# First FFN of a diffusion backbone: five of seven modulation sums move from TensorE to trees of accumulating DMAs

## The chip, the cores and the metric

One core of one Trainium2 chip. The metric is the device time in microseconds of one execution of the whole program. TensorE is called PE, VectorE DVE, ScalarE ACT, GpSimd POOL and SyncE SP, as in the profile.

## The reference

Two layers over 256 latent tokens (`x`) and, in layer 0, 256 context tokens (`ctx`); width 1024, FFN width 2816. Each layer is a half-step SwiGLU FFN, a token mixer (neighbourhood attention, then a short convolution) and a second FFN. Everything is FP32. Cut to what the change touches:

```python
m  = (silu(c)     @ ada_w[i] + ada_b[i]).reshape(B, 9, 1, D)   # nine modulation vectors for x
mc = (silu(c_ctx) @ ada_w[i] + ada_b[i]).reshape(9, D)         # and for ctx
# half-step FFN, with shift, scale, gate = m[:, 0], m[:, 1], m[:, 2]
a, u = split((x * (1 + scale) + shift) @ w_in, 2)
y = (silu(a) * u) @ w_out
x = layer_norm(alpha * x + 0.5 * gate * y) * g + b
```

`ada_w[i]` is 1024 x 9216, so the two layers' modulation weights are large, and each is used for a matrix by vector product only.

## The kernel before

**Matmuls.** An FP32 product is made of three passes on PE: weights and activations are each split into a high part (`...h`, rounded to fp32r) and the rest (`...l`), and high x high, low x high and high x low are summed. A weight unit of 512 KB arrives by SP's DMA (`w1r`, `w2r`, `wqr`), ACT copies it to the high part (L216, `w1h`), DVE subtracts to get the low part (L219, `w1l`), each in two halves. The split tiles rotate through five buffers; in the first FFN `ext = [1, 0]` adds a sixth (`whx`, `wlx`).

**First FFN (25 to 398 us).** The 22 blocks of 128 FFN columns come in panels of mostly two blocks; a panel of two blocks has four weight units, each with two of the eight k slices for both gate halves. Three parts follow each other: panels 0 to 3, 4 to 7, 8 to 10. In a part each block j is computed by `f0_mm` (L729): first all k for gate half z = 0, then all k for z = 1; then `f0_gate` (ACT's silu, DVE's product `sil` and the split `gh`, `gl`). After the part's panels, `out_gemm` multiplies by `w_out` (`w2` units, n outside, then the four token tiles t, then units), and DVE adds each result bank to `xt` (`res`, then `x` or `xc`). After the third part comes the layer norm, whose `rs` GpSimd computes (L435, L436), and the attention's query weights `wq`.

**The modulation stream.** `ada(vecs)` computes 14 more modulation vectors in seven groups of two, in the background of the first FFN. For each k slice SP loads `ar` (512 KB, L316), and DVE multiplies by the condition's column and accumulates in `acc` (128 partitions x 1024; L305 first, L307 then), one accumulator for x and one for ctx, or one for each of two vectors. At the end of a group PE sums over the partitions with a matrix `ones` (L342), DVE adds the bias rows (L343, `adar`), and SP stores the rows in `scr` in DRAM (L345), from where later stages load them as `gate` or `mrow`. How fast the stream moves is set by `tick()`, which PE's program calls after pieces of work: it adds the rate `background[1]` to a counter and runs a step of the stream for each whole one. PE's instructions keep the order of the program; for the other engines a scheduler sets it, `queued`, `issue_after` and priorities bind it in places.

**Later groups** (`on_pool`) are summed by GpSimd's PARTITION_ALL_REDUCE and one small DMA to `scr` (L356, L357), five times after 700 us.

Of the kernel before, what the change touches and what calls it, by code (L numbers as in the profile page):

```python
# [10 lines left out]
F32 = mybir.dt.float32  # L11
# [3 lines left out]
ALU = mybir.AluOpType  # L15
# [16 lines left out]
S2 = 7  # L32
WB = (4, 5, 5)
PB = {"mm": 3, "at": 3, "tp": 2}
W_EARLY = 40
ADA_SLOW, ADA_FAST, ADA_SLOWEST = 3, 0.6, 0.13
KT_IDLE = 6
BIAS_AT = 24
ADA_LATE = 20
ADA_LAG = 1  # L40
# [28 lines left out]
E0 = (0,)  # L69
E2 = (0, 5, 7)  # L70
HOLD = 4
SUM_AT = (2, 4, 6, 7, 8)


@with_exitstack
def backbone_kernel(
# [6 lines left out]
    nc = tc.nc  # L83
    sync = nc.sync
# [4 lines left out]
    sp = ctx.enter_context(tc.tile_pool(name="sp", bufs=2))  # L89
# [3 lines left out]
    hp = phase.__enter__()  # L93
# [1 line left out]
    uid = [0]  # L95
    w_early = [0]
    last_split, last_lo = [], []
    ext = [1, 0]
    ada_late = [0]

    def nm(s):
        uid[0] += 1
        return f"{s}_{uid[0]}"
# [7 lines left out]
    def mmb(s="mm", t=0):  # L111
        return bank("at" if t % 2 else "mm", s)
# [11 lines left out]
    background = [None, 0.0, 0.0]  # L124
# [24 lines left out]
    def tick(n=1):  # L149
        clock[0] += n  # L150
        for w in [w for w in waiting if w.due <= clock[0]]:
            w.get()
        background[2] += background[1] * n
        while background[0] is not None and background[2] >= 1:
            background[2] -= 1
            bg_step()
# [122 lines left out]

    for z in mrow:  # L280
        nc.gpsimd.memset(z, 0.0)
    bias_rows = []
    on_pool = [False]
    sums, last_gate = [], []
    gate_ins = []

    def ada(vecs):


        acc = {}  # L290

        def accumulate(l, m, k, w):
            with ExitStack() as st:
                for i in gate_ins + (last_lo if on_pool[0] else []):
                    st.enter_context(tc.issue_after(i.ins))
                for i, vec in enumerate(vecs):
                    if vec[:2] != (l, m):
                        continue
                    if k == 0:
                        acc[i] = hp.tile([P, D], F32, tag="acc", bufs=2, name=nm("acc"))  # L300
                    sc = cst[:, k, vec[2]:vec[2] + 1]
                    for h in range(2):
                        src, a = (c[:, h * 512:(h + 1) * 512] for c in (w, acc[i]))
                        if k == 0:
                            nc.vector.tensor_scalar(a, src, sc, None, op0=ALU.mult)  # L305
                        else:
                            nc.vector.scalar_tensor_tensor(out=a, in0=src, scalar=sc, in1=a,  # L307
                                                           op0=ALU.mult, op1=ALU.add)
            if on_pool[0] and k == KC - 1:
                sums.extend((vec, acc[i]) for i, vec in enumerate(vecs) if vec[:2] == (l, m))  # L310

        loaded = []
        for l, m in dict.fromkeys((l, m) for l, m, _ in vecs):
            for k in range(KC):
                w = hp.tile([P, D], F32, tag="ar", bufs=3, name=nm("ar"))
                sync.dma_start(w, ada_w[l, k * P:(k + 1) * P, m * D:(m + 1) * D])  # L316
                loaded.append((l, m, k, w))
                if len(loaded) > (ADA_LAG if gate_ins else 0):
                    accumulate(*loaded.pop(0))
                yield 1  # L320
        while loaded:
            accumulate(*loaded.pop(0))
            if loaded:
                yield 1
        if on_pool[0]:
            return
        n = 2 * len(vecs)
        if not bias_rows:
            bias_rows.append(hp.tile([P, 512], F32, tag="adab", name=nm("adab")))
            nc.gpsimd.memset(bias_rows[0], 0.0)  # L330
        bt = bias_rows[0]
        for i, (l, m, v) in enumerate(vecs):
            sync.dma_start(bt[64 * i:64 * i + 64:32], ada_b[l, m * D:(m + 1) * D].rearrange("(a b) -> a b", b=512))
        yield 1
        yield 1
        yield 1
        rows = hp.tile([P, 512], F32, tag="adar", name=nm("adar"))
        ps = tpb("ada")
        for i in range(len(vecs)):
            for h in range(2):  # L340
                j = 2 * i + h
                nc.tensor.matmul(ps[32 * j:32 * j + 32, :], ones, acc[i][:, h * 512:(h + 1) * 512], start=True, stop=True)  # L342
        nc.vector.tensor_tensor(out=rows[:32 * n], in0=ps[:32 * n], in1=bt[:32 * n], op=ALU.add)  # L343
        for i, (l, m, v) in enumerate(vecs):
            sync.dma_start(scr[l][v, m * D:(m + 1) * D].rearrange("(a b) -> a b", b=512),  # L345
                           rows[64 * i:64 * i + 64:32, :])
        yield 1

    def sum_up():
# [11 lines left out]
    made = [0]  # L361
# [53 lines left out]
    def residual(ps, xt, gate, wgt, alpha, stats=None, behind=()):  # L415

        t = sp.tile([P, 512], F32, tag="tmp", bufs=3, name=nm("res"))[:, 0:ps.shape[1]]
        with queued(behind[0:1]):
            nc.vector.scalar_tensor_tensor(out=t, in0=ps, scalar=wgt, in1=gate, op0=ALU.mult, op1=ALU.mult)
        with queued(behind[1:2]):  # L420
            if alpha is None:
                nc.vector.tensor_tensor(out=xt, in0=xt, in1=t, op=ALU.add)
            else:
                nc.vector.scalar_tensor_tensor(out=xt, in0=xt, scalar=alpha, in1=t, op0=ALU.mult, op1=ALU.add)
            if stats is not None:
                nc.vector.bn_stats(stats, xt)
# [74 lines left out]
    def run(gen):  # L501
        for _ in gen:
            pass
# [91 lines left out]


    w_in, w_out = ffn_w_in[0, 0], ffn_w_out[0, 0]
    ab0 = hp.tile([P, D], F32, tag="acc", bufs=2, name="ab0")
    nc.vector.memset(ab0, 0.0)
    nc.scalar.dma_start(ab0[2:64:32], ada_b[0, 0:2 * D].rearrange("(m b) -> m b", m=2))  # L600
    xt = []
# [11 lines left out]
    def start_tile():  # L613
        nar[0] += 1
        if nar[0] % 5 in (2, 4):
            return hp.tile([P, 2, 512], F32, tag="pt", bufs=4, name=nm("ar")).rearrange("p a b -> p (a b)")
        return hp.tile([P, D], F32, tag="ar", bufs=3, name=nm("ar"))

    marks = []

# [115 lines left out]
    def f0_gate(bk):  # L736
        t = sp.tile([P, 512], F32, tag="s2", bufs=S2, name=nm("sil0"))
        nc.scalar.activation(t, bk[0], AF.Silu)
        nc.vector.tensor_tensor(out=t, in0=t, in1=bk[1], op=ALU.mult)
        hi, lo = act(F32R, "gh"), act(F32R, "gl")  # L740
        split(t, hi, lo)
        return hi, lo
# [32 lines left out]
    for fh, (p0, p1) in enumerate(parts):  # L775
        gT = []
        for p in range(p0, p1):
            units = u0 if p == 0 else [f0_unit(p, u) for u in range(KC // F0_KN[F0[p][1]])]
            for j in range(F0[p][1]):
                if p == 0:  # L780
                    bk = b0[j]
                else:
                    bk = []
                    for z in range(2):
                        bk.append(mmb("f0", z))
                        for k in range(0, KC, 2):
                            f0_mm(bk[z], p, units, j, z, (k, k + 1))
                            tick()
                gT.append(f0_gate(bk))
        if fh == 0:  # L790
            for v in range(2):
                big = hp.tile([P, 2, 512], F32, tag="pt", bufs=4, name=nm("gate"))
                sync.dma_start(big.rearrange("p a b -> p (a b)"),
                               bass.AP(scr[0].tensor, scr[0][v, 2 * D:3 * D].offset, [[0, P], [1, D]]))
                gates.append([big[:, 0], big[:, 1]])
            background[1] = 0.44
        elif fh == 1:
            ada_late[0] = ADA_LATE

# [281 lines left out]
    hp = phase.__enter__()  # L1081
# [35 lines left out]
    for i in range(len(steps) + LAG + V_LAG):  # L1117
# [14 lines left out]
        n = int(credit)  # L1132
# [28 lines left out]
    phase = tc.tile_pool(name="ph2", bufs=1)  # L1161
    hp = phase.__enter__()
    on_pool[0] = True
    sync.dma_start(scr[1][0, 4 * D:9 * D].rearrange("(a b) -> a b", a=16), ada_b[1, 4 * D:9 * D].rearrange("(a b) -> a b", a=16))
    ext[0] = 2

    v0 = made[0]
# [128 lines left out]
```

## Time and profile before

| | |
|---|---|
| median of 3 runs | 1244.49 us (1244.3 to 1245.33) |
| profiled execution | 1246.53 us |
| its span, first to last instruction | 1244.7 us |
| granted clock | 0.998 |
| PE busy | 1225.9 us, 98% |
| DVE busy | 965.2 us, 78% |
| ACT busy | 643.7 us, 52% |
| POOL busy | 81.6 us, 7% |
| DMA | 275.67 MB, mean 221 GB/s |

The span is cut into stretches in what follows; a stretch's row gives the busy time of each engine in it, and where PE's equals the stretch's length, PE has not waited there. A line such as `L307 DVE ... x266 | 186.6, 747 | 12.3 <-DMA ar` is a group of instructions: busy time, mean ns of one, idle time of the engine just before them and what ended it. Row "a <- b: 10.3, 7, 3.3" of the waits says that an engine waited at a for b: total us, times, longest. Times within PE's timeline are starts; the ends of matmuls overlap.

### The profile page before, as it was taken

To read this page: it belongs to the slowest core of one execution; us is meant where nothing else is said; L and a number is where in the kernel's file an instruction comes from. 1 tells how busy PE (TensorE), PEld (TensorE's weight loads), DVE (VectorE), ACT (ScalarE), POOL (GpSimd) and SP (SyncE) were. 2 spreads that over 40 slices of the span, in tenths; PEclk is the share of its full clock that TensorE was granted. 3 is DMA by queue.
4 is the path that set the end of the run, shared out by engine and by line. 5 is a ranking of instruction groups with operands and counts; after the bars stand their busy time and mean duration, and the time that the engine had idled before them with its cause. 6 is when DMAs were issued, how large, how long until landed. Compare 5 with 4: busy or idle time off the path is not lost.

```text
span 1244.7 us, 17236 instructions
## 1 busy us (share of the span) xinstructions
PE 1225.9 (98%) x5794; PEld 995.3 (80%) x5794; DVE 965.2 (78%) x1675; ACT 643.7 (52%) x1233; POOL 81.6 (7%) x93
## 2 busy tenths in 40 slices
PE   8999999999999999999999999999999999999997
PEld 5787778778778878777788888888888887888886
DVE  3698987888878867888877677878867798768746
ACT  2433132321325566687777635668645644678631
POOL 0000000000001011120000020020200110000200
PEclk9999999999999999999999999999999999999999
DMA  9986679778852654554899957879886765799851
GB/s 294 305 249 228 177 235 298 259 253 289 285 187 68 179 116 95 121 111 128 264 296 311 269 202 242 231 231 324 246 286 225 220 220 153 204 279 277 245 186 68
DMA packets 232304, 275.67 MB, mean 221 GB/s; under 512 B 59622, under 2 KB 178910, under 8 KB 232216
## 3 DMA queue, kind: packets, MB, share of 16 engines
q1 hardware_dynamic: 232020, 274.54, 73.0%
q8 instruction: 45, 0.74, 0.2%
q14 instruction: 43, 0.35, 0.1%
q0 software_dynamic: 160, 0.02, 0.1%
q10 hardware_dynamic: 36, 0.02, 0.0%
HBM read 265.27 MB, written 2.20 MB: 215 GB/s over the span
## 4 chain that ended last, share of the span: by engine, by line
PE 90%; DVE 4%; DMA 3%; ACT 2%; issue 1%; SPq 0%; POOL 0%; DVEq 0%; ACTq 0%
PE f L729 19%; PE w L170 17%; PE w L171 17%; PE w L173 17%; PE wkv L170 3%; PE wkv L171 2%; PE wkv L173 2%; DMA ar<-in_ada_w_dram 1%; PE wc L170 1%; PE wc L171 1%; PE wc L173 1%; PE S L1026 1%; PE o L1064 1%; PE hT L454 1%; PE PT L1051 1%
## 5 line engine op out<-in xcount | busy, mean ns | idle before, releaser
L219 DVE TENSOR_TENSOR w1l<-w1r,w1h 128x512 fp32r<-128x512 f32 (+1 forms) x352 | 232.0, 704 | 44.5 <-ACT w1h L216 43.6
L216 ACT ACTIVATE w1h<-w1r 128x512 fp32r<-128x512 f32 (+1 forms) x352 | 198.2, 617 | 112.0 <-DMA w1r<-in_ffn_w_in_dram 40.8
L170 PE MATMUL w<-w1h,hTh 128*128 128x512 f32 x528 | 206.3, 391 | 1.2 <-ACT hTh L118 1.2
L171 PE MATMUL w<-w1l,hTh 128*128 128x512 f32 x528 | 205.6, 389 | 0.0
L307 DVE SCALAR_TENSOR_TENSOR acc<-ar,cst,acc 128x512 f32<-128x512 f32 x266 | 186.6, 747 | 12.3 <-DMA ar<-in_ada_w_dram 11.9
L170 PE MATMUL w<-w2h,gh 128*128 128x512 f32 (+1 forms) x446 | 173.3, 389 | 0.0
L171 PE MATMUL w<-w2l,gh 128*128 128x512 f32 (+1 forms) x446 | 172.2, 387 | 0.0
L216 ACT ACTIVATE w2h<-w2r 128x512 fp32r<-128x512 f32 x176 | 101.3, 624 | 135.5 <-PE w L173 95.0
L173 PE MATMUL w<-w1h,hTl 128*128 128x512 f32 x528 | 162.6, 389 | 0.0
L219 DVE TENSOR_TENSOR w2l<-w2r,w2h 128x512 fp32r<-128x512 f32 x176 | 117.7, 710 | 57.6 <-ACT w2h L216 56.7
L173 PE MATMUL w<-w2h,gl 128*128 128x512 f32 (+1 forms) x446 | 136.1, 386 | 0.0
L729 PE MATMUL f<-h0h,w1h 128*128 128x512 f32 x352 | 132.4, 392 | 1.9 <-ACT w1h L216 1.5
L729 PE MATMUL f<-h0l,w1h 128*128 128x512 f32 x352 | 133.0, 391 | 0.0
L729 PE MATMUL f<-h0h,w1l 128*128 128x512 f32 x352 | 132.8, 390 | 0.0
L170 PEld LDWEIGHTS w<-w1h,hTh 128*128 128x128 f32 x528 | 99.1, 188 | 22.5 <-ACT hTh L118 2.1
L173 PEld LDWEIGHTS w<-w1h,hTl 128*128 128x128 f32 x528 | 99.0, 188 | 20.9 <-DVE hTl L119 0.4
L171 PEld LDWEIGHTS w<-w1l,hTh 128*128 128x128 f32 x528 | 99.2, 188 | 20.6 <-DVE w1l L219 0.3
L170 PEld LDWEIGHTS w<-w2h,gh 128*128 128x128 f32 x446 | 83.8, 188 | 19.2 <-issue 1.7
L171 PEld LDWEIGHTS w<-w2l,gh 128*128 128x128 f32 x446 | 83.8, 188 | 16.9 <-DVE w2l L219 0.3
L173 PEld LDWEIGHTS w<-w2h,gl 128*128 128x128 f32 x446 | 83.3, 188 | 17.1
L729 PEld LDWEIGHTS f<-h0h,w1h 128*128 128x128 f32 x352 | 65.7, 188 | 19.5 <-issue 3.4
L729 PEld LDWEIGHTS f<-h0l,w1h 128*128 128x128 f32 x352 | 65.6, 188 | 14.2 <-issue 0.8
(197 smaller groups left out, 1763.6 us busy)
## 6 DMA issues: line engine op xcount, KB each, us to landing
w1r<-in_ffn_w_in_dram SPq DMA_DIRECT2D x340, 256.0 KB
ar<-in_ada_w_dram SPq DMA_DIRECT2D x128, 512.0 KB
w2r<-in_ffn_w_out_dram SPq DMA_DIRECT2D x88, 512.0 KB
ar<-in_ada_w_dram SPq DMA_DIRECT2D x32, 256.0 KB
wkvr<-in_na_w_qkv_dram SPq DMA_DIRECT2D x32, 256.0 KB
wcr<-in_sc_w_in_dram SPq DMA_DIRECT2D x32, 256.0 KB
wqr<-in_na_w_qkv_dram SPq DMA_DIRECT2D x8, 512.0 KB
wor<-in_na_w_out_dram SPq DMA_DIRECT2D x8, 512.0 KB
```

The source lines that it names most:

```text
L170: nc.tensor.matmul(ps, lh, rh, start=first and i == 0, stop=False)
L171: nc.tensor.matmul(ps, lh, rl, start=False, stop=False)
L173: nc.tensor.matmul(ps, ll, rh, start=False, stop=last and i == n - 1)
L216: last_split[:] = [nc.scalar.activation(hi[:, a:a + m // W_HI], raw[:, a:a + m // W_HI], AF.Copy)]
L219: last_lo[:] = [nc.vector.tensor_tensor(out=lo[:, a:b], in0=raw[:, a:b], in1=hi[:, a:b].bitcast(F32), op=ALU.subtract)]
L307: nc.vector.scalar_tensor_tensor(out=a, in0=src, scalar=sc, in1=a, op0=ALU.mult, op1=ALU.add)
L454: nc.tensor.transpose(ps[:, k * P:(k + 1) * P], z[h][:, k * P:(k + 1) * P], ident)
L729: nc.tensor.matmul(ps, w, hT0[k][part == 1], start=(k == part == 0), stop=(k == KC - 1 and part == 1))
L1026: nc.tensor.matmul(banks[i], (qh, ql, qh)[f][ps, qs], (kh, kh, kl)[f][ps, :], start=f == 0, stop=f == 2)
L1051: nc.tensor.transpose(pt[:, k * P:(k + 1) * P], pr[:, k * P:(k + 1) * P], ident)
L1064: nc.tensor.matmul(ps, v[k][:, s], p[:, k], start=k == part == 0, stop=part == 1 and k == 3)
```

## The change

- `BY_TREE = (1, 2, 3, 4, 5)`: the five middle groups are no longer summed by PE. GpSimd issues DMAs that add the upper half of an accumulator's partitions to the lower half (64, 32, ... 1), and an eighth that adds the one row left to `scr`. Groups 0 and 6 stay on PE; a DVE copy takes the bank, and GpSimd's DMA adds it to `scr`.
- The biases are written to `scr` ahead of the stream by three DRAM to DRAM copies of SP, so the bias tile and DVE's additions go.
- `acc` gets four buffers instead of two, `ar` four instead of three; the sixth split buffer goes (`ext = [0, 0]`).
- In f0 the k pairs are outside and the gate halves inside, so that both banks end together. In the last block of each part the stream's rate is 0.
- The stream's rates: `ADA_FAST` .64 for .6, .4 for .44 after part 0; accumulations are bound to come after the latest residual or gate product on DVE (`pace`).
- Behind the last tree GpSimd drains.

```diff
-ADA_SLOW, ADA_FAST, ADA_SLOWEST = 3, 0.6, 0.13
+ADA_SLOW, ADA_FAST, ADA_SLOWEST = 3, 0.64, 0.13
+BY_TREE = (1, 2, 3, 4, 5)
-    ext = [1, 0]
+    ext = [0, 0]
...
-                for i in gate_ins + (last_lo if on_pool[0] else []):
+                for i in gate_ins + (last_lo if on_pool[0] else pace):
...
-                        acc[i] = hp.tile([P, D], F32, tag="acc", bufs=2, name=nm("acc"))
+                        acc[i] = hp.tile([P, D], F32, tag="acc", bufs=2 if on_pool[0] else 4, name=nm("acc"))
...
-            if on_pool[0] and k == KC - 1:
-                sums.extend((vec, acc[i]) for i, vec in enumerate(vecs) if vec[:2] == (l, m))
+            if k == KC - 1:
+                ready = [(vec, acc[i]) for i, vec in enumerate(vecs) if vec[:2] == (l, m)]
+                if on_pool[0]:
+                    sums.extend(ready)
+                elif made[0] in BY_TREE:
+                    n = P // 2
+                    while n:
+                        for _, a in ready:
+                            nc.gpsimd.dma_start(a[0:n], a[n:2 * n], accum_op=ALU.add)
+                        n //= 2
+                    for (l, m, v), a in ready:
+                        last = nc.gpsimd.dma_start(scr[l][v:v + 1, m * D:(m + 1) * D], a[0:1], accum_op=ALU.add)
+                    if made[0] == BY_TREE[-1] and (l, m) == vecs[-1][:2]:
+                        with tc.issue_after(last.ins):
+                            nc.gpsimd.drain()
...
-                w = hp.tile([P, D], F32, tag="ar", bufs=3, name=nm("ar"))
+                w = hp.tile([P, D], F32, tag="ar", bufs=3 if on_pool[0] else 4, name=nm("ar"))
...
-        rows = hp.tile([P, 512], F32, tag="adar", name=nm("adar"))
+        for _ in range(3 if made[0] else 2):
+            yield 1
+        if made[0] in BY_TREE:
+            return
+        rows = sp.tile([P, 512], F32, tag="s2", bufs=S2, name=nm("adar"))
...
-        nc.vector.tensor_tensor(out=rows[:32 * n], in0=ps[:32 * n], in1=bt[:32 * n], op=ALU.add)
+        nc.vector.tensor_copy(rows, ps)
         for i, (l, m, v) in enumerate(vecs):
-            sync.dma_start(scr[l][v, m * D:(m + 1) * D].rearrange("(a b) -> a b", b=512),
-                           rows[64 * i:64 * i + 64:32, :])
+            nc.gpsimd.dma_start(scr[l][v, m * D:(m + 1) * D].rearrange("(a b) -> a b", b=512),
+                                rows[64 * i:64 * i + 64:32, :], accum_op=ALU.add)
...
+    for l, v, r in ((0, 0, slice(2 * D, 9 * D)), (0, 1, slice(2 * D, 5 * D)), (1, 0, slice(0, 9 * D))):
+        sync.dma_start(scr[l][v, r].rearrange("(a b) -> a b", a=16), ada_b[l, r].rearrange("(a b) -> a b", a=16))
...
-                    bk = []
-                    for z in range(2):
-                        bk.append(mmb("f0", z))
-                        for k in range(0, KC, 2):
+                    rate, end = background[1], p == p1 - 1 and j == F0[p][1] - 1
+                    if end:
+                        background[1] = 0.0
+                    bk = [mmb("f0", z) for z in range(2)]
+                    for k in range(0, KC, 2):
+                        for z in range(2):
                             f0_mm(bk[z], p, units, j, z, (k, k + 1))
                             tick()
+                    if end:
+                        background[1] = rate
...
-            background[1] = 0.44
+            background[1] = 0.4
```

Three places show how instructions move. The first is GpSimd's whole program of the first FFN: before, nothing stands between setting up `mrow` and the layer norm's `rs` of the FFN's end.

```order
L281 MEMSET mrow_87 128x128
L330 MEMSET adab_926 128x512
L1175 MEMSET srow 128x128
L435 TENSOR_TENSOR rs_3347<-mv_3345,lnc 128x1
L436 TENSOR_TENSOR rs_3347<-rs_3347,lnc 128x1
```

After (the first rows of the first pair of trees, of 82 rows in all ahead of `rs`; `adar_962` is group 0, `acc_999` and `acc_1002` are group 1):

```order
L352 DMA scr_118<-adar_962 2x512 x2
L317 DMA acc_999<-acc_999 64x1024
L317 DMA acc_1002<-acc_1002 64x1024
L317 DMA acc_999<-acc_999 32x1024
L317 DMA acc_1002<-acc_1002 32x1024
L317 DMA acc_999<-acc_999 16x1024
```

The two trees of a group alternate on the queue, each DMA behind the one that it reads from.

The second place is DVE's queue around the first trees: where group 1's accumulators are complete, before (`acc_998`, `acc_1001`; the sum over partitions is PE's, the bias addition `adar` follows on DVE):

```order
L307 SCALAR_TENSOR_TENSOR acc_1001<-ar_1211,cst,acc_1001 128x512 x2
L419 SCALAR_TENSOR_TENSOR res_1237<-w_203_1204,gate_1128 128x512
L219 TENSOR_TENSOR w2l_1315<-w2r_1313,w2h_1314 128x512
L424 SCALAR_TENSOR_TENSOR x_128<-x_128,res_1237 128x512
L219 TENSOR_TENSOR w2l_1315<-w2r_1313,w2h_1314 128x512
```

And after, the end of the same accumulations in the output GEMM's first half, and then the first use of a slot that a tree has held (`acc_1729` takes the slot of `acc_999`):

```order
L220 TENSOR_TENSOR w2l_1354<-w2r_1352,w2h_1353 128x512 x2
L307 SCALAR_TENSOR_TENSOR acc_999<-ar_1255,cst,acc_999 128x512 x2
L307 SCALAR_TENSOR_TENSOR acc_1002<-ar_1255,cst,acc_1002 128x512 x2
L426 SCALAR_TENSOR_TENSOR res_1366<-w_212_1317,gate_1111 128x512
...
L746 TENSOR_TENSOR sil_258_1662<-sil_258_1662,f_257_1593 128x512
L305 TENSOR_SCALAR acc_1729<-ar_1719,cst 128x512 x2
L120 TENSOR_TENSOR gl_1666<-sil_258_1662,gh_1665 128x512
```

Group 1 now ends later, behind the first four results of the output GEMM, and group 3's accumulator waits for group 1's tree instead of PE.

The third place is DVE's queue at the end of the FFN, where `wql` are the low parts of the first query weights; before:

```order
L119 TENSOR_TENSOR hTl_3454<-h_3452,hTh_3453 128x512
L419 SCALAR_TENSOR_TENSOR res_3487<-w_572_3440,gate_1130 128x512
L219 TENSOR_TENSOR wql_3583<-wqr_3581,wqh_3582 128x512
L119 TENSOR_TENSOR hTl_3468<-h_3466,hTh_3467 128x512
L422 TENSOR_TENSOR xc_131<-xc_131,res_3487 128x512
L219 TENSOR_TENSOR wql_3583<-wqr_3581,wqh_3582 128x512
L426 BN_STATS st_3293<-xc_131 128x6
L219 TENSOR_TENSOR wkvl_3663<-wkvr_3661,wkvh_3662 128x512
L433 BN_AGGR mv_3491<-st_3293 128x2
```

After:

```order
L220 TENSOR_TENSOR wql_3592<-wqr_3590,wqh_3591 128x512
L440 BN_AGGR mv_3456<-st_3283 128x2
L453 TENSOR_SCALAR xc_130<-xc_130,mv_3456,rs_3458 128x512 x2
L120 TENSOR_TENSOR hTl_3477<-h_3475,hTh_3476 128x512
L426 SCALAR_TENSOR_TENSOR res_3510<-w_561_3463,gate_1113 128x512
...
L433 BN_STATS st_3316<-xc_131 128x6
L220 TENSOR_TENSOR wql_3592<-wqr_3590,wqh_3591 128x512
L440 BN_AGGR mv_3514<-st_3316 128x2
L220 TENSOR_TENSOR wql_3606<-wqr_3604,wqh_3605 128x512
L453 TENSOR_SCALAR xc_131<-xc_131,mv_3514,rs_3516 128x512 x2
L220 TENSOR_TENSOR wql_3606<-wqr_3604,wqh_3605 128x512
```

Before, one of the four units is split here (`wql_3583`), after two (`wql_3592`, `wql_3606`), the last half of the second behind the normalization of `xc_131`.

More of the change, by code (lines that the diff above doesn't have):

```diff
@@ L281, in backbone_kernel @@
         nc.gpsimd.memset(z, 0.0)
-    bias_rows = []
     on_pool = [False]
     sums, last_gate = [], []
-    gate_ins = []
+    gate_ins, pace = [], []
     def ada(vecs):
@@ L314, in ada @@
             for k in range(KC):
-                w = hp.tile([P, D], F32, tag="ar", bufs=3, name=nm("ar"))
+                w = hp.tile([P, D], F32, tag="ar", bufs=3 if on_pool[0] else 4, name=nm("ar"))
                 sync.dma_start(w, ada_w[l, k * P:(k + 1) * P, m * D:(m + 1) * D])
                 loaded.append((l, m, k, w))
-                if len(loaded) > (ADA_LAG if gate_ins else 0):
+                if len(loaded) > ADA_LAG:
                     accumulate(*loaded.pop(0))
@@ L326, in ada @@
             return
[L327 to L336, printed above, removed]
-        rows = hp.tile([P, 512], F32, tag="adar", name=nm("adar"))
+        for _ in range(3 if made[0] else 2):
[3 more added lines that the diff above has]
+        rows = sp.tile([P, 512], F32, tag="s2", bufs=S2, name=nm("adar"))
         ps = tpb("ada")
@@ L418, in residual @@
         with queued(behind[0:1]):
-            nc.vector.scalar_tensor_tensor(out=t, in0=ps, scalar=wgt, in1=gate, op0=ALU.mult, op1=ALU.mult)
+            pace[:] = [nc.vector.scalar_tensor_tensor(out=t, in0=ps, scalar=wgt, in1=gate, op0=ALU.mult, op1=ALU.mult)]
         with queued(behind[1:2]):
@@ L597, in backbone_kernel @@
     w_in, w_out = ffn_w_in[0, 0], ffn_w_out[0, 0]
-    ab0 = hp.tile([P, D], F32, tag="acc", bufs=2, name="ab0")
+    ab0 = hp.tile([P, D], F32, tag="acc", bufs=2 if on_pool[0] else 4, name="ab0")
     nc.vector.memset(ab0, 0.0)
@@ L616, in start_tile @@
             return hp.tile([P, 2, 512], F32, tag="pt", bufs=4, name=nm("ar")).rearrange("p a b -> p (a b)")
[L617 removed]
+        return hp.tile([P, D], F32, tag="ar", bufs=4, name=nm("ar"))
     marks = []
@@ L738, in f0_gate @@
         nc.scalar.activation(t, bk[0], AF.Silu)
-        nc.vector.tensor_tensor(out=t, in0=t, in1=bk[1], op=ALU.mult)
+        pace[:] = [nc.vector.tensor_tensor(out=t, in0=t, in1=bk[1], op=ALU.mult)]
         hi, lo = act(F32R, "gh"), act(F32R, "gl")
@@ L1163, in backbone_kernel @@
     on_pool[0] = True
-    sync.dma_start(scr[1][0, 4 * D:9 * D].rearrange("(a b) -> a b", a=16), ada_b[1, 4 * D:9 * D].rearrange("(a b) -> a b", a=16))
     ext[0] = 2
```

## The prediction

> **What bounds the kernel now.** I read first a table of stretches cut at the phases of the first FFN, because the change lies between 49 and 415 us. Columns: stretch, its length, busy time of PE, PEld, DVE, ACT and POOL, granted clock, DMA share, GB/s.
>
> ```profile
> 49.00:98.00 49.00, 49.00 (x220) 40.22 (x222) 43.06 (x71) 20.30 (x37) 0.00 (x0) 1.00 0.76 239
> 98.00:137.00 39.00, 39.00 (x179) 30.78 (x172) 36.03 (x58) 11.63 (x20) 0.00 (x0) 1.00 0.67 216
> 137.00:161.00 24.00, 24.00 (x107) 19.85 (x106) 23.75 (x40) 5.48 (x10) 0.00 (x0) 1.00 0.68 198
> 161.00:272.00 111.00, 111.00 (x500) 89.09 (x499) 89.77 (x144) 31.20 (x55) 0.00 (x0) 1.00 0.80 261
> 272.00:296.00 24.00, 24.00 (x108) 19.87 (x107) 22.59 (x37) 6.49 (x12) 0.00 (x0) 1.00 0.88 287
> 296.00:373.00 77.00, 77.00 (x347) 61.89 (x346) 59.65 (x96) 21.91 (x38) 0.00 (x0) 1.00 0.75 245
> 373.00:390.00 17.00, 17.00 (x79) 14.10 (x79) 13.67 (x30) 3.46 (x6) 0.76 (x2) 1.00 0.29 94
> 390.00:415.00 25.00, 25.00 (x129) 20.89 (x128) 22.25 (x42) 23.01 (x54) 2.93 (x7) 1.00 0.26 60
> ```
>
> PE is busy in every microsecond of the eight stretches, at granted clock 1.00; GpSimd does nothing until 373. So here PE's own work is the time, and every PE instruction taken out shortens the span, as long as DVE (up to 99% busy in 137:161) and ACT (92% in the last stretch) still deliver operands in time. The chain that ended last says the same and gives the beat:
>
> ```profile
> 48.82 48.99 PE f L729 x216
> 97.81 1.00 PE ada L342 x8
> ...
> 314.74 1.00 PE ada L342 x8
> ```
>
> 48.99 / 216 = .2268 us per FFN matmul. L342 is the modulation sum, on the chain. Its true cost is read from the starts around it in PE's timeline:
>
> ```profile
> 97.42 0.39 PE L729 MATMUL f<-h0l,w1h 128*128 128x512 f32 x1
> 97.74 1.07 PE L342 MATMUL ada<-acc,ones 128*32 128x512 f32 x8
> 98.74 0.50 PE L729 MATMUL f<-h0h,w1h 128*128 128x512 f32 x1
> 99.07 0.39 PE L729 MATMUL f<-h0h,w1l 128*128 128x512 f32 x1
> ...
> ```
>
> **The change part by part.** From 97.42 the third following FFN matmul should start .2268 x 3 = .68 later; PE's next rows settle that:
>
> ```profile
> 99.31 0.39 PE L729 MATMUL f<-h0l,w1h 128*128 128x512 f32 x1
> ```
>
> 99.31 − 97.42 − .68 = 1.21 us for one group's sum.
>
> *Five sums leave PE.* 5 x 1.21 = −6.05 us, nothing beside it, since PE never waits there. The low end is the chain's own 1.00 each: −5.0. Their rows in the table of groups, with what else goes:
>
> ```profile
> L342 PE MATMUL ada<-acc,ones 128*32 128x512 f32 x56 | 7.5, 604 | 0.0
> L343 DVE TENSOR_TENSOR adar<-ada,adab 128x512 f32<-128x512 f32 x7 | 4.8, 684 | 0.0
> L307 DVE SCALAR_TENSOR_TENSOR acc<-ar,cst,acc 128x512 f32<-128x512 f32 x266 | 186.6, 747 | 12.3 <-DMA ar<-in_ada_w_dram 11.9
> L305 DVE TENSOR_SCALAR acc<-ar,cst 128x512 f32<-128x512 f32 x38 | 16.9, 482 | 8.1 <-PE ada L342 6.5 <-DMA ar<-in_ada_w_dram 1.6
> ```
>
> DVE loses five bias additions (5 x .68 = 3.4 us) and its 6.5 us of waits for PE's sums; SP loses the small stores and gains three bias copies ahead of the stream. All that lies beside PE: 0.
>
> *Eighty accumulating DMAs on GpSimd.* Nothing of that size exists before; the nearest rows are the five 4 KB DMAs that GpSimd issues later: the group, its line of the DMA table, and the smallest, middle and largest time from issue to landing.
>
> ```profile
> L357 POOL DMA_DIRECT2D scr<-red x5 | 5.1, 1022 | 1.5 <-POOL red L356 1.5
> scr<-red POOLq DMA_DIRECT2D x5, 4.0 KB, 3.1
> DMA to landing us min/median/max: 2.3/3.1/4.5
> ```
>
> A tree is a chain of eight such DMAs, each waiting for the one before. By the median 8 x 3.1 = 25 us; the low end 8 x 2.3 = 18; the high end, with the 1.02 of issue added to the slowest landing, 8 x 5.5 = 44. I take 25 plus 2 us per tree for bytes: the steps move 256 + 128 + ... + 4, some 512 KB, at the stretch's 261 GB/s. Two trees of a group alternate on the queue (2 x 1.02 of issue fits into 3.1), so a pair takes about 30.
>
> Who waits for a tree? GpSimd has nothing else queued; its next work is the layer norm's `rs`, and it waited 382 us for that:
>
> ```profile
> POOL rs L435 <- DVE mv L433: 396.3, 4, 382.3
> ```
>
> The last tree's inputs are done near 314 (where the sixth sum stands in the chain above), so trees and drain end by about 345, at the high end 360: no delay. Nearest in time is DVE: with four `acc` slots, group 3's first accumulation takes the slot of group 1's first tree. The order puts group 1's last accumulations ahead of the residual of `x_127`, and that first accumulation behind the gate multiplication of panel 4's second block. In the trace of before these neighbours run here:
>
> ```profile
> 145.32 0.69 DVE L419 SCALAR_TENSOR_TENSOR res<-w,gate 128x512 f32<-128x512 f32 x1
> 184.49 0.69 DVE L739 TENSOR_TENSOR sil<-sil,f 128x512 f32<-128x512 f32 x1
> ```
>
> The tree has 184.5 − 145.3 = 39 us; 30 needs no wait, 44 makes DVE 5 us late. PE is not hurt by that at once: DVE has then about 7 us of work to the next weight half, which belongs to the panel after the next, and a panel lasts 96 x .2268 = 21.8 us. I count 8 us of cover. So 0 here; DVE waits from 4.9 us a step, PE from 47 / 8 = 5.9. The other reuses come later behind their trees, and SP's reload `mrow` only delays `ar` loads whose slots aren't free yet.
>
> Here the Trainium skill speaks against the change: "SBUF — State Buffer", section "SBUF: two separate sides", says that a DVE instruction using both shared ports keeps GpSimd from writing its descriptors, and its section on bandwidth intuition gives a DMA of .62 us becoming 3.1. If every step paid that difference of 2.5 us, a tree would need 8 x (3.1 + 2.5) = 45 us by an estimate from that page, 6 late for DVE and still inside the cover, so the sum would stay. No run here shows it.
>
> *Block order in f0, and the pause.* Both gate halves now end together, and a unit of weights (k pair, both halves) is needed every 12 x .2268 = 2.7 us and not all four in the first half block. With five split buffers the next panel's unit may be written as the old one is left, one block (10.9 us) ahead. Cost 0, covered by that lead. The pause moves accumulations away from each part's last block and piles them into the output GEMM, where DVE is 99% busy: walking the order through the rows, the last `w2l` before the first boundary is ready about 1 us before its use. Group 0's PE sum stands 12 matmuls (2.7 us) earlier than 97.74, at 95.0. DVE's rows there:
>
> ```profile
> 86.06 2.74 DVE L307 SCALAR_TENSOR_TENSOR acc<-ar,cst,acc 128x512 f32<-128x512 f32 x4
> 93.84 0.69 DVE L739 TENSOR_TENSOR sil<-sil,f 128x512 f32<-128x512 f32 x1 [2.64 <-PE f L729]
> ```
>
> Where four accumulations stood, the order now has nine: 86.06 + 9 x .67 = 92.1, and the idle 2.64 takes them; a late load may make it 94.3. These two I bound by 0 and +1 us each and take 0.
>
> *The sixth split buffer goes.* That bites where the next stage begins. ACT's splits of the first query weights, then DVE's row of that time, then PE's uses (each a timeline):
>
> ```profile
> 377.38 1.15 ACT L216 ACTIVATE wqh<-wqr 128x512 fp32r<-128x512 f32 x2 [13.22 <-PE w L173]
> 380.10 1.16 ACT L216 ACTIVATE wqh<-wqr 128x512 fp32r<-128x512 f32 x2 [0.20 <-ACT wqh L216]
> 398.26 0.66 ACT L216 ACTIVATE wqh<-wqr 128x512 fp32r<-128x512 f32 x1
> ```
> ```profile
> 395.96 0.21 DVE L433 BATCH_NORM_AGGREGATE mv<-st 128x2 f32<-128x12 f32 x1
> 398.02 0.68 DVE L119 TENSOR_TENSOR hTl<-h,hTh 128x512 fp32r<-128x512 f32 x1
> 401.03 0.68 DVE L219 TENSOR_TENSOR wql<-wqr,wqh 128x512 fp32r<-128x512 f32 x1
> 402.83 0.20 DVE L433 BATCH_NORM_AGGREGATE mv<-st 128x2 f32<-128x12 f32 x1
> 404.29 1.00 DVE L446 TENSOR_SCALAR xc<-xc,mv,rs 128x512 f32<-128x512 f32 x2 [0.71 <-POOL rs L436]
> ```
> ```profile
> 402.28 0.39 PE L171 MATMUL wq<-wql,hTh 128*128 128x512 f32 x1
> 403.64 0.39 PE L171 MATMUL wq<-wql,hTh 128*128 128x512 f32 x1
> ```
>
> Before, three units are split near 380 and the fourth late, done 401.7, needed 403.64 (403.19 for its first half). After, only two fit; units three and four go through DVE's crowded end. By the order DVE does a half of unit three ahead of the aggregate at 395.96, which pushes what follows by .6: `hTl` at 398.62, residual 399.22, `xc` 399.94, `hTl` 400.55, statistics 401.16, second half of unit three 401.77 to 402.45 (needed 402.28: .17 late), aggregate 402.37, first half of unit four 402.49 to 403.17, then `xc` normalization, which waits for GpSimd as before (404.29 − 402.83 = 1.46): 403.83 to 404.75, and behind it the second half of unit four, ready 405.43. Needed 403.64 + .17, so PE waits 1.6 more: +1.8 us in all. The ends: +.2 if that normalization doesn't hold the split, +3 if ACT, 92% busy here, is late too. Nothing later gives it back, since PE is the bound again behind it.
>
> **The sum.** −6.05 + 0 + 0 + 1.8 = −4.25 us. On the profiled execution, 1246.53 us (span 1244.7), that is 1242.3; it stood 2.04 above the median of the runs, and the chosen forecast is the median's, 1244.49 − 4.25 = 1240.2.
>
> **The rivals.** (a) *No new stall*: the tail's late split is absorbed. For it: the late unit four of before did no harm. Against: the walk above is 1.6 late. Time 1244.49 − 6.05 = 1238.4.
>
> (b) *The other side: slow trees.* A step costs over 4.9 us, DVE stops at group 3's first accumulation with the next panel's gate and splits queued behind it, and over 5.9 PE stops too. For it: a landing of 4.5 exists among only five samples, all of 4 KB, while a first step is 64 times that and shares the DMA engines with a stream at .80. Against: the median 3.1, and the steps soon shrink to 4 KB. The change turns to a loss at (47 + 4.25) / 8 = 6.4 us a step; at 7 us the tree ends 17 us after its place, 9 past the cover: −4.25 + 9 = +4.8, 1249.2. The Trainium skill's port rule (page and section above) would be one way to it, in part: its 5.6 alone stays below 5.9.
>
> (c) *Many small stalls.* All upper ends come true at once: +1 at group 0's sum, +1 at the first boundary, +3 at the tail: −6.05 + 5 = −1.05, 1243.4. For it: DVE's 23.75 of 24 and one split buffer less. Where DVE stands in such stretches its waits say:
>
> ```profile
> DVE res L419 <- PE w L173: 10.3, 7, 3.3
> ```
>
> Against: seven times, up to 3.3 us, DVE was at the output GEMM's results before PE had them, so it has some lead there.
>
> **Chances and range.** Steps of .2% (2.5 us) are about what a measurement here tells from no change. The forecast (−3 to −5.5, so 1239 to 1241.5) .48; (a) .20; (c) .20; (b) .12. Faster by over 2.5 us: all of the forecast and of (a), a quarter of (c) and a little of (b): .48 + .20 + .05 + .01 = .74. Same: .13 of (c) and .03 of (b) .16. Slower: .02 + .08 = .10. The range must leave out no more than 2 in 10: low 1237.8 (below (a) for a second gain, such as the waits of DVE that vanish), high 1244.5, which holds (c) and stops short of (b).
>
> **What the profile after would show.** PE rows of the sum 16, not 56, and starts around them 6 us less in all by 390; the wait that shows the tail right is PE on DVE `wql` of 1.5 to 2 us about 398; trees: issues to landing near 3, DVE's `acc` never waiting for a GpSimd DMA. Wrong would be: DVE waits at the `acc` row near 180 of over 8 us; PE waits in 90:300; or a landing over 5.9 at the first steps.

## The result and the profile after

The change made the kernel slower: 1259.28 us median (1256.69 to 1260.82, 4 runs) against 1244.91 (1244.3 to 1245.46), ratio 1.0113 with a 95% interval of [1.0095, 1.0131]. The forecast was 1240.2, with a range up to 1244.5. The profiled execution took 1256.69, with a span of 1254.9 (before 1244.7), so the account below explains these 10.2 us of span, and not the whole 14.4 by which the medians differ.

Where PE stands at the same work, read from the starts in its two timelines:

| PE starts | before | after | difference |
|---|---|---|---|
| FFN blocks after the start-up | 48.57 | 46.86 | −1.7 |
| output GEMM of part 0 | 116.56 | 114.86 | −1.7 |
| panels of part 1 | 161.30 | 158.38 | −2.9 |
| output GEMM of part 1 | 250.80 | 245.42 | −5.4 |
| panels of part 2 | 295.54 | 288.94 | −6.6 |
| output GEMM of part 2 | 363.14 | 354.22 | −8.9 |
| fold of the modulation columns, `mcT` | 371.44 | 368.99 | −2.5 |
| first transposes `hT` | 389.38 | 395.72 | +6.3 |
| query product `wq` | 397.99 | 406.89 | +8.9 |
| transposes of the queries `qT` | 413.42 | 424.01 | +10.6 |

Down to 354 us the sums leave as forecast: each that left PE shows as 1.2 (group 6's sum, which now stands later, is in the −8.9 too). The 1.7 of the start-up were not forecast. All runs below start PE's blocks .3 to 1.8 earlier than the one profile of before, which itself took 1.6 us more than its median; so this may belong to that execution and not to the change. Then 19.5 us are lost within 70, 1.2 of them group 6's sum at its new place. The stretches (columns as before) show it as idle PE and as a lower clock, and GpSimd, idle there before, at work:

```profile
161.00:272.00 111.00, 111.00 (x492) 91.90 (x491) 92.70 (x149) 32.37 (x56) 30.72 (x38) 1.00 0.88 286
...
296.00:373.00 77.00, 73.81 (x313) 59.94 (x312) 58.53 (x101) 20.55 (x36) 18.47 (x23) 0.96 0.85 264
373.00:390.00 17.00, 15.32 (x71) 11.42 (x69) 10.47 (x17) 3.46 (x6) 3.96 (x5) 1.00 0.11 11
390.00:415.00 25.00, 17.93 (x79) 14.71 (x80) 16.00 (x30) 15.07 (x36) 5.08 (x10) 0.80 0.24 81
```

PE's waits in that time are three (engine, line, for whom; us in total, times, longest):

```profile
PE hT L461 <- DVE x L453: 7.4, 1, 7.4
PE w L171 <- ACT gh L119: 3.2, 1, 3.2
PE wq L172 <- DVE wql L220: 1.4, 1, 1.4
```

The third is the late query split that the prediction had at 1.8. The two others come from GpSimd's queue. Its DMAs by size, with the median time from issue to landing:

```profile
acc<-acc POOLq DMA_DIRECT2D x10, 256.0 KB, 7.2
acc<-acc POOLq DMA_DIRECT2D x10, 128.0 KB, 4.7
...
acc<-acc POOLq DMA_DIRECT2D x10, 4.0 KB, 4.7
```

The median step costs 4.7 where the prediction had 3.1, and below 256 KB it hardly gets shorter with its size: 4 KB take as long as 128. GpSimd's timeline shows how these steps fill the queue (last bracket: idle before, and what ended it):

```profile
141.76 0.84 POOL L317 DMA_DIRECT2D acc<-acc  x1 [43.99 <-DVE acc L307]
...
323.33 0.80 POOL L317 DMA_DIRECT2D acc<-acc  x1 [4.65 <-DMA acc<-acc]
328.99 0.81 POOL L317 DMA_DIRECT2D acc<-acc  x1 [4.86 <-DMA acc<-acc]
334.38 0.80 POOL L317 DMA_DIRECT2D acc<-acc  x1 [4.57 <-DMA acc<-acc]
...
379.50 0.79 POOL L317 DMA_DIRECT2D acc<-acc  x1 [2.12 <-DMA acc<-acc]
382.07 0.80 POOL L317 DMA_DIRECT2D acc<-acc  x1 [1.79 <-DMA acc<-acc]
384.37 0.78 POOL L320 DMA_DIRECT2D scr<-acc  x1 [1.50 <-DMA acc<-acc]
392.41 1.71 POOL L352 DMA_DIRECT2D scr<-adar  x2 [7.26 <-issue]
393.58 0.77 POOL L442 TENSOR_TENSOR rs<-mv,lnc 128x1 f32<-128x1 f32 x1
```

From 141.8 to 384.4 the 80 DMAs follow each other without a break for other work, one in 3.07 us on average, since two trees overlap only in part. A step is 5.4 to 5.7 us long while the stream is loading (323 to 334, DMA share .94 there), and 2.3 to 2.6 when the stream is over (379 to 384). Behind the last one the drain holds the queue for 7.26, and only then come group 6's DMAs and the layer norm's `rs`. What DVE sees of it:

```profile
312.16 1.41 DVE L307 SCALAR_TENSOR_TENSOR acc<-ar,cst,acc 128x512 f32<-128x512 f32 x2
...
319.51 0.88 DVE L305 TENSOR_SCALAR acc<-ar,cst 128x512 f32<-128x512 f32 x2 [5.35 <-DMA w1r<-in_ffn_w_in_dram]
...
345.31 0.91 DVE L305 TENSOR_SCALAR acc<-ar,cst 128x512 f32<-128x512 f32 x2 [9.01 <-DMA scr<-acc]
...
359.56 0.68 DVE L746 TENSOR_TENSOR sil<-sil,f 128x512 f32<-128x512 f32 x1
...
385.10 0.21 DVE L440 BATCH_NORM_AGGREGATE mv<-st 128x2 f32<-128x12 f32 x1
395.03 1.00 DVE L453 TENSOR_SCALAR x<-x,mv,rs 128x512 f32<-128x512 f32 x2 [9.72 <-POOL rs L443]
```

An L305 row of two begins a new accumulator, and 14 L307 follow it. So group 5 is complete at 313.6 (the first row), and 319.51 and 345.31 begin the first and the second accumulator of group 6. Twice DVE clearly waits for GpSimd: 9.0 us at group 6's second accumulator, for the slot of group 4's second tree, which ends at 345, with the gates of the last blocks queued behind it; and 9.7 for `rs`. The 5.35 us at 319.51 are probably a third wait of this kind: the instruction doesn't read `w1r`, and it takes the slot of group 4's first tree, whose last DMA is issued at 314.04 and lands at 319.0. PE's rows are the end of the two clear ones:

```profile
361.19 0.80 PE L171 MATMUL w<-w2h,gh 128*128 128x512 f32 x1 [3.19 <-ACT gh L119]
361.79 0.63 PE L172 MATMUL w<-w2l,gh 128*128 128x512 f32 x1
362.22 1.05 PE L174 MATMUL w<-w2h,gl 128*128 128x512 f32 x2
...
395.72 1.94 PE L461 MATMUL hT<-ident,x 128*128 128x128 f32 x8 [7.40 <-DVE x L453]
```

Behind the first wait the FFN matmuls start .43 us apart (361.79 to 362.22) for some 5.7 us, where .2268 is usual. So a wait of 3.2 us cost 6.5 by the table (−8.9 to −2.5), and the wait of 7.4 cost 10.1 beside the sum of 1.2 (−2.5 to +8.9).

### The profile page after: what moved, and what is told of

It is laid out like the page before. It is cut to its first block, busy times and chain, and to the rows that moved or that the text cites. A ratio compares the mean times of both kernels' runs of the same rounds, so it can differ in the third digit from the quotient of the medians.

```text
span 1254.9 us, 17279 instructions
## 1 busy us (share of the span) xinstructions
PE 1224.9 (98%) x5754; PEld 998.5 (80%) x5754; DVE 956.3 (76%) x1670; ACT 644.8 (51%) x1233; POOL 148.5 (12%) x176
## 4 chain that ended last, share of the span: by engine, by line
PE 64%; DMA 17%; issue 8%; DVE 7%; POOL 2%; ACT 1%; SPq 1%; DVEq 0%; POOLq 0%; ACTq 0%
PE w L171 15%; PE w L174 15%; PE w L172 14%; DMA acc<-acc 13%; PE f L736 3%; PE wkv L171 2%; PE wkv L172 2%; PE wkv L174 2%; DVE acc L307 1%; DMA ar<-in_ada_w_dram 1%; PE wc L171 1%; PE wc L174 1%; PE wc L172 1%; PE S L1039 1%; DMA wcr<-in_sc_w_in_dram 1%
## 5 line engine op out<-in xcount | busy, mean ns | idle before, releaser
L307 DVE SCALAR_TENSOR_TENSOR acc<-ar,cst,acc 128x512 f32<-128x512 f32 x266 | 189.1, 758 | 13.5 <-DMA ar<-in_ada_w_dram 13.5
L220 DVE TENSOR_TENSOR w2l<-w2r,w2h 128x512 fp32r<-128x512 f32 x176 | 113.3, 687 | 57.2 <-ACT w2h L217 56.3
L317 POOL DMA_DIRECT2D acc<-acc x70 | 57.3, 844 | 210.3 <-DMA acc<-acc 165.6
```

Source lines behind the costliest of these rows:

```text
L220: last_lo[:] = [nc.vector.tensor_tensor(out=lo[:, a:b], in0=raw[:, a:b], in1=hi[:, a:b].bitcast(F32), op=ALU.subtract)]
L317: nc.gpsimd.dma_start(a[0:n], a[n:2 * n], accum_op=ALU.add)
```

## The experiments

The theory was: the step length under load times the number of steps fills GpSimd's queue until after the layer norm needs it, and a slot is held too long on the way. The rivals: the drain, DVE keeping GpSimd from writing descriptors, and the rest of the change (five split buffers, block order, pause, rates).

**The drain taken out.**

```diff
-                    if made[0] == BY_TREE[-1] and (l, m) == vecs[-1][:2]:
-                        with tc.issue_after(last.ins):
-                            nc.gpsimd.drain()
```

> The change without GpSimd's drain behind the last tree. Theory (GpSimd's queue): in the changed kernel the 80 tree DMAs run one behind another until 384.4 us, then the drain holds the queue from 385.15 to 392.41, so the layer norm's rs starts at 393.6 and PE waits 7.4 us for it. Without the drain rs starts at about 386, PE's wait falls below 1.5 us, and the time falls by 6 to 9 us, to about 1251. Rival (the trees alone hold rs, the drain only shows a wait that comes anyway): rs stays near 392 and the time within 2 us of 1259.

1253.28 us, ratio 1.0076 [1.0061, 1.0092]: 6.0 less than the change. The trees end as late as before, and `rs` follows at once (GpSimd's timeline, then PE's wait):

```profile
385.81 0.77 POOL L320 DMA_DIRECT2D scr<-acc  x1 [1.49 <-DMA acc<-acc]
...
387.48 1.06 POOL L439 TENSOR_TENSOR rs<-mv,lnc 128x1 f32<-128x1 f32 x1
```
```profile
PE hT L458 <- DVE x L450: 2.4, 1, 2.4
```

PE's wait falls from 7.4 to 2.4, not below 1.5 as the theory had it: the queue is itself late. So the drain is 6 of the 14 us, and the rest is not the drain.

**A stream with little traffic.** One `ar` tile in eight is loaded and used eight times.

```diff
-                w = hp.tile([P, D], F32, tag="ar", ...)
-                sync.dma_start(w, ada_w[l, k * P:(k + 1) * P, m * D:(m + 1) * D])
+                if on_pool[0] or not kept or k % 8 == 0:
+                    w = hp.tile([P, D], F32, tag="ar", ...)
+                    sync.dma_start(w, ada_w[l, k * P:(k + 1) * P, m * D:(m + 1) * D])
+                    kept[:] = [w]
+                w = kept[0]
```

> The change, but in the first FFN only one ar tile in eight is loaded and then used eight times (the result is not the reference's); DVE's work and the trees are unchanged, the stream's traffic falls by 7/8. Theory (a tree step's length is the landing of its DMA under the load of SP's stream): steps of 4.7 us in the middle fall to 2.5 to 3.2, as they are in the changed kernel at 373 to 384 us where the DMA engines are 0.1 to 0.25 busy; the last tree ends 50 us earlier, the waits for the accumulator slot and for rs go, time 1238 to 1242. Rival (DVE's instructions keep GpSimd from writing descriptors): the steps stay at 4.5 to 5, the last tree ends near 380, time 1255 or more.

1240.74 us, ratio 0.9969 [0.9957, 0.9981]. GpSimd's DMAs and the stretch of part 1:

```profile
acc<-acc POOLq DMA_DIRECT2D x10, 256.0 KB, 3.9
...
acc<-acc POOLq DMA_DIRECT2D x10, 4.0 KB, 2.1
```
```profile
337.14 0.77 POOL L320 DMA_DIRECT2D scr<-acc  x1 [1.48 <-DMA acc<-acc]
```
```profile
161.00:272.00 111.00, 111.00 (x491) 91.92 (x490) 92.83 (x149) 32.62 (x56) 35.44 (x44) 1.00 0.55 144
```

DVE works as much as in the change (92.83 against 92.70 us), the DMA share falls from .88 to .55, and the steps fall to 2.1 to 3.9; the median of all is 3.1, just the prediction's price. The last tree issues its last DMA at 337, where the prediction had trees and drain end by 345. No slot is waited for, and `rs` costs DVE the 2.0 us in two waits that it cost before, with the drain still there; the time is what the prediction had forecast for the real kernel. From the start-up (47.41) to the queries' transposes (407.97) PE gains 4.3 us on before, and the sum had 4.25. So this run shows that the stream's traffic is what lengthens the steps, and that the other terms together were right. By what part of their way the DMAs are slowed was not separated. The run leaves out work, so it is no version to use.

**Another kind of DVE instruction.** All accumulations are written as products alone.

```diff
-                        if k == 0:
+                        if k == 0 or not on_pool[0]:
                             nc.vector.tensor_scalar(a, src, sc, None, op0=ALU.mult)
```

> The change, but every accumulation of the first FFN is written as the first one is, a product without the sum (the result is not the reference's): 224 TENSOR_SCALAR of 482 ns where there were 196 SCALAR_TENSOR_TENSOR of 747 and 28 TENSOR_SCALAR. Traffic of the stream is unchanged. Theory (a tree step's length is the landing of its DMA under the stream's load): steps in 161:272 stay within 10% (median landing 4.8, all steps). Rival (a DVE instruction of the TENSOR_SCALAR kind keeps GpSimd from writing descriptors): eight times as many of them, the median step is longer by half a microsecond or more, and GpSimd's own issue time (0.80 us) grows.

1259.96 us (two runs), ratio 1.012 [1.010, 1.014]. DMAs by size, the stretch of part 1, and then the longest row of GpSimd's timeline with DVE's row beside it:

```profile
acc<-acc POOLq DMA_DIRECT2D x10, 256.0 KB, 6.9
...
acc<-acc POOLq DMA_DIRECT2D x10, 4.0 KB, 4.8
```
```profile
161.00:272.00 111.00, 111.00 (x492) 91.90 (x490) 75.00 (x150) 32.60 (x56) 34.04 (x37) 1.00 0.89 286
```
```profile
162.51 4.82 POOL L317 DMA_DIRECT2D acc<-acc  x2 [2.26 <-DMA acc<-acc]
```
```profile
161.56 6.46 DVE L305 TENSOR_SCALAR acc<-ar,cst 128x512 f32<-128x512 f32 x16
```

Eight times the TENSOR_SCALAR, and 18 us less DVE work in the stretch: the median landing of all steps is 4.6 against 4.8, GpSimd's median issue .82 against .80. So neither DVE's kind of instruction nor how busy it is sets the usual step. But the longest issue is 4.00 us, the first of the two at 162.51, beside sixteen TENSOR_SCALAR in a row, and another, at 292.28, takes 2.41 beside six; in the change, where at most three follow each other while trees run, the longest is 1.24. The rule of the Trainium skill that the prediction weighed ("SBUF — State Buffer", section "SBUF: two separate sides", descriptors starved by a two-port DVE instruction) would have it so, and shows here in two of seventy issues; it does not account for the steps of the change.

**A fifth slot.** `acc` five buffers, `ar` three.

```diff
-... tag="acc", bufs=2 if on_pool[0] else 4 ...
+... tag="acc", bufs=2 if on_pool[0] else 5 ...
-... tag="ar", bufs=3 if on_pool[0] else 4 ...
+... tag="ar", bufs=3 ...
```

> The change with five acc slots instead of four, and three ar tiles instead of four to make room. Theory (GpSimd's queue): group 6's first accumulator no longer waits 9.0 us for the slot of group 4's second tree, so DVE is not held there, PE's wait of 3.2 us for the last part's first results and the slower clock behind it go (6.6 us between the part's first output matmul and the fold of the modulation columns); the trees and the drain still end near 392, and the wait for rs grows by up to what PE has gained, since rs is bound to GpSimd and not to PE: time between 1252 and 1259. Rival (the two losses are independent): the whole 6.6 come back, 1252 or less.

1259.49 us, ratio 1.0114 [1.0095, 1.0133], just above the theory's upper end of 1259; PE's wait for `gh` falls from 3.2 to .5, and

```profile
PE hT L461 <- DVE x L453: 16.8, 1, 16.8
```

All that PE gained it waits at the layer norm instead. The slot wait is real, but behind it stands the end of GpSimd's queue, which is bound to the DMAs and not to PE.

**Fewer trees.** `BY_TREE = (1, 2, 3)`, the rest as in the change.

> Trees for groups 1, 2 and 3 alone; groups 4 and 5 are summed by PE again, with a DVE copy and one accumulating DMA each as groups 0 and 6. Theory (GpSimd's queue): the last tree lands near 280 us and the drain ends near 290, 90 us before rs; no accumulator slot is waited for, so PE loses neither the 3.2 us at the last part's first results nor the 7.4 us at the layer norm. Three sums less on PE (-3.6), the late query split stays (+1.4): 1244.9 - 2.2 = 1242.7. Rival (the loss comes from the rest of the change: five split buffers, block order, pause, rates): PE still waits at the part boundaries, 1250 or more.

1244.16 us, ratio 0.9992 [0.9983, 1.0]. The last tree's last DMA (GpSimd), and PE's waits up to the attention's scores:

```profile
280.01 0.78 POOL L320 DMA_DIRECT2D scr<-acc  x1 [4.15 <-DMA acc<-acc]
```
```profile
PE S L1039 <- DVE kTl L120: 1.6, 1, 1.6
PE wq L172 <- DVE wql L220: 1.3, 1, 1.3
```

No wait for GpSimd is left, and the rival (the rest of the change) is refuted at 1250 or more. It is not the 1242.7 either: beside the query split, 1.6 us are lost at the attention's keys.

**No trees**, with the change's rates, and then with `ADA_FAST` .72 instead of .64.

```diff
-BY_TREE = (1, 2, 3, 4, 5)
+BY_TREE = ()
```

> No trees at all: all seven groups are summed by PE, each followed by a DVE copy and one accumulating GpSimd DMA; block order, pause, rates and buffers are those of the changed kernel. Theory (GpSimd's queue): no gain and no wait on GpSimd, only the late query split: 1244.9 + 1.4 = 1246.3. Rival (the rest of the change loses the time): 1252 or more.

> No trees, as in the run that took 1253.2, but the stream's fast rate .72 instead of .64. There PE waited 2.4 us at 389 for the last group's accumulators, and the clock fell behind that. Theory (the changed rates fit a stream that is shorter by a step for each tree; with seven PE sums it is late): that wait goes and the time is 1244 to 1247. Rival (block order and the lost buffer cost that time): 1250 or more.

1253.2 us (ratio 1.0062 [1.0048, 1.0076]), a miss by 7, and 1249.76 (1.0038 [1.0024, 1.0052]). The first run's wait, and the second's:

```profile
PE ada L349 <- DVE acc L307: 2.4, 1, 2.4
```
```profile
PE ada L349 <- DVE acc L307: 0.7, 1, 0.7
```

Behind the second stands this part of PE's timeline, group 5's sum and the matmul after it:

```profile
317.69 1.05 PE L349 MATMUL ada<-acc,ones 128*32 128x512 f32 x4
319.42 1.71 PE L349 MATMUL ada<-acc,ones 128*32 128x512 f32 x4 [0.68 <-DVE acc L307]
321.06 0.50 PE L736 MATMUL f<-h0h,w1h 128*128 128x512 f32 x1
```

A group summed by PE takes one step of the stream more than one summed by a tree, so at the change's rates the last group is late at PE. A faster rate gives about half of it back. It remains 3.5 above the 1246.3 that the query split alone explains. Most of that is a late accumulation again: group 5's sum holds PE from 317.69 to 321.06, 3.4 us where 1.0 is usual. The last 1 of the 3.5 us stays open.

**The sixth split buffer back, at the price of a slot.** Three trees, `ext = [1, 0]`, three `acc` and three `ar` tiles.

> Trees for groups 1, 2 and 3, and the sixth split buffer back (three acc slots and three ar tiles make room). Theory (the tail's late query split comes from the lost buffer): PE's wait for wql of 1.3 us, seen with three trees and five buffers, goes, and the time falls from 1244.2 to about 1242.8; three slots hold as long as group 2's second tree lands before group 4 begins. Rival (a slot short): DVE waits at an acc for a tree for over 8 us, 1246 or more.

1260.28 us, ratio 1.0122 [1.0107, 1.0137]. DVE's longest account:

```profile
DVE acc L305 <- DMA scr<-acc: 17.6, 2, 11.2
```

The rival was right: with three slots the trees hold DVE even when they are few. Slots and the step length belong together.

**The buffers where the stream leaves them.** The last two `w2` units take an `acc` and an `ar` slot each; no drain; three trees, four, and four with five `acc` slots.

```diff
+        nwq[0] += s == "w2"
+        if s == "w2" and nwq[0] in (21, 22):
+            hi = hp.tile([P, D], F32, tag="acc", ...).bitcast(F32R)
+            lo = hp.tile([P, D], F32, tag="ar", ...).bitcast(F32R)
```

> Trees for groups 1, 2 and 3, no drain, and the last two w2 units of the first FFN split into tiles of the stream that are idle by then (one acc and one ar slot each), so that two more of the five rotating buffers are free for the first query weights. Theory (the late wql comes from the lost sixth buffer, and nothing else of the change costs time with three trees): all four query units are split before 385, PE's wait of 1.3 us for wql goes, 1244.2 - 1.3 = 1242.9. Rival (the wait moves: DVE is full there whatever the buffers): PE waits as long for another operand and the time stays at 1244.

> The same with four trees (groups 1 to 4). Theory (GpSimd's queue): one PE sum less again, but group 4's second tree still ends near 340 and group 6's first accumulator needs its slot near 336, so DVE waits some 5 to 9 us there: 1241.7 if PE's lead covers it, 1246 to 1248 if PE waits for gh again. Rival (the queue is not at its limit with four trees): no wait at the slot, 1241.7.

> The same four trees with five acc slots and three ar tiles. Theory (GpSimd's queue): the slot wait goes, nothing of the queue is near rs (the last tree ends before 345), five buffers and late loads cost little: 1244.9 - 4 x 1.21 = 1240.1. Rival (three ar tiles starve DVE, as its waits for ar of 22.6 us with five trees suggest): PE waits for splits behind late accumulations, 1244 or more.

Three trees: 1244.7 us against 1245.33 beside it, ratio 0.9990 [0.9981, 0.9999]. PE's wait for `wql` is gone, but its sum of group 6 now holds a wait of about 1.2 (PE's timeline; 1.0 is usual):

```profile
373.88 2.30 PE L350 MATMUL ada<-acc,ones 128*32 128x512 f32 x8
```

So the wait moved, as the rival said. With plain three trees (ratio .9992) this is the fastest complete version of the study; the two can't be told apart, and both are within what the prediction called no change. Four trees: 1253.82 (1.0065 [1.0051, 1.0079]), and with five slots 1250.31 (1.0042 [1.0029, 1.0054]), both worse than the theory had them. Of four trees DVE's wait at the slot, with PE's behind it (PE also waits 3.8 us for a `w2h`), and of five slots DVE's wait for loads:

```profile
DVE acc L309 <- DMA scr<-acc: 6.7, 1, 6.7
```
```profile
PE w L171 <- ACT gh L119: 5.8, 1, 5.8
```
```profile
DVE acc L311 <- DMA ar<-in_ada_w_dram: 20.4, 20, 5.3
```

The fourth tree is already one too many for four slots, and the tile that a fifth costs seems missing from the loads: DVE's waits for `ar` were 13.5 us in the change.

**GpSimd's reduction in place of the trees.**

```diff
+                        red = hp.tile([P, D], F32, tag="red", name=nm("red"))
+                        nc.gpsimd.partition_all_reduce(red, a, P, ReduceOp.add)
+                        last = nc.gpsimd.dma_start(scr[l][...], red[0:1], accum_op=ALU.add)
```

> The change with GpSimd's PARTITION_ALL_REDUCE and one accumulating 4 KB DMA for each vector of groups 1 to 5 in place of its tree (as later groups are summed), no drain, three acc slots instead of four and one tile for the sum. Theory (GpSimd's queue): ten reductions of 6.3 us and DMAs that no step waits for make some 75 us of queue instead of 243, so no slot and no rs is waited for, and PE is rid of five sums: 1244.9 - 6.05 + 1.4 = 1240.2. Rival (DVE and GpSimd hold each other up when both read SBUF): DVE's accumulations beside a reduction get longer, PE waits at the part boundaries, 1246 or more.

1256.78 us, ratio 1.0096 [1.0081, 1.0111]: the rival. GpSimd is in time, but DVE pays (one reduction, the DVE instruction beside it, and DVE's group in 137:350, where the change has 482 ns):

```profile
180.66 10.15 POOL L316 PARTITION_ALL_REDUCE red<-acc  x1 [20.45 <-DVE acc L307]
```
```profile
184.75 5.02 DVE L307 SCALAR_TENSOR_TENSOR acc<-ar,cst,acc 128x512 f32<-128x512 f32 x1
```
```profile
L305 DVE TENSOR_SCALAR acc<-ar,cst 128x512 f32<-128x512 f32 x18 | 32.6, 1848 | 1.1 <-DMA ar<-in_ada_w_dram 1.1
```

PE waits 9.5 us for `w1l` behind that. A port rule shows here plainly. "SBUF — State Buffer", section "Who interferes with whom", of the Trainium skill says that a DVE instruction in a two-port mode, or with two inputs in SBUF, and a GpSimd instruction that reads SBUF exclude each other for a whole instruction. These rows agree in that one holds the other up; they don't show it for the whole instruction, since six `w1l` splits of DVE (181.14 to 184.83) ran at their usual length inside the reduction's 10.15 us.

## Why the prediction was wrong

- *Five sums leave PE, −6.05.* Right: the table's steps are 1.2 each, and with little traffic the whole change took 1240.74.
- *A tree takes 25 us plus 2, a pair 30, trees and drain end by 345, at the high end 360.* This is the step that failed: the price of a step, and through it the end of the queue. The step is 4.7 (5.4 to 5.7 under full load), not 3.1: the price came from five DMAs that GpSimd issued at other times, each with nothing of its kind around it, and the rise under load was bounded by bytes, while it is there for 4 KB too. So a tree of groups 3 and 4 takes 41 to 42 us from its first issue to its last landing. The queue was not summed at all: 79 x 3.07 = 243 us from the first to the last of the 80 issues. Only the trees of groups 1 and 2 alternate in pairs; in groups 3 to 5 each vector has its own loads, so their trees come one by one, and each first DMA stands behind all but the last few of the tree before. A vector of these groups is complete every 22 us (203 to 314), but a tree starts only every 28 (219 to 360, by the sizes in the trace), so the delay grows from 16 us to 46. The inputs were in time: group 5 is complete at 313.6, as the prediction had it near 314. But its last tree starts at 360.0, and its last DMA is issued at 384.4, 39 us later than taken. At the assumed price the missing sum would have done no harm: with little traffic, at a median of 3.1, the same queue issues its last DMA at 337.
- *The drain.* Taken as nothing in that sentence; it holds the queue 7.3 us, and without it the time is 6.0 less.
- *Who waits for a tree?* I looked at the first reuse of a slot, which has 39 us, and said that the others come later. There DVE did not wait. It waited at the last reuse, 9.0 us, and probably 5.3 at the one before, because the queue's lateness adds up from tree to tree.
- *Rival (b)* was the right side, but by its own rule (a loss from 6.4 us a step) it would not have come at 4.7: it looked at one tree's length and not at the queue's end.
- *Block order and pause: 0.* The late parts that I bounded by 1 us each don't show: PE's starts lose nothing up to 354.
- *The sixth buffer, +1.8.* Right in place and size: PE's starts lose 1.7 there (+8.9 to +10.6), 1.4 of it in one wait. That its removal makes the kernel faster was not shown: with the buffers back, the wait was found at group 6's sum.
- *What a wait costs.* No term had the clock behind a wait, about 3 us each at the two long ones.

## What to carry to other kernels

When work is moved to an idle engine as a chain of dependent DMAs, price a step by its latency under the load that the other queues have at that time, multiply by all the steps that one queue must issue, and compare the queue's end with the next thing that the engine owes; the length of one chain says little. Look at the last user of a recycled buffer, not at the first. An idle GpSimd is not free for reductions either, where DVE is nearly full.

## What the runs showed of the hardware

- An accumulating GpSimd DMA of 4 KB landed in 4.7 us at a DMA share of about .9 and in 2.1 where the share was .43 to .73; one of 256 KB in 7.2 and 3.9 (medians).
- GpSimd's drain behind the last tree held its queue 7.26 us in the change and in the two runs with its trees, its drain and full traffic, and 4.65 behind three trees; the same place without it took none.
- Beside sixteen TENSOR_SCALAR in a row on DVE one DMA issue of GpSimd took 4.00 us, beside six 2.41; .80 is usual.
- After 3.2 us without work PE's matmuls started .43 us apart instead of .2268 for some 5.7 us (granted clock .66 in 360:370). In the run without the drain a wait of 2.5 us did the same (.72 in 360:366), one of 2.4 did not (1.00 in 390:396), and the waits of 1.3 to 1.4 at `wql` left the clock at 1.00. The Trainium skill, "TensorE: Matmul & The Clock Gate", section "What's actually happening", puts the limit at about 3.4 us of idle time and half the rate until about as much busy time has passed. The trace agrees in the rate; here 2.5 us sufficed once, and the slow stretch behind the 3.2 was 5.7 us long.
